# Attention scores over 128 rows: zero-padded queries in the memory of the residual

## The chip, the cores and the metric

The kernel runs on one core of a Trainium2 chip. The metric is the device time of one launch, in microseconds. Three runs of the kernel before took 1101.29, 1101.87 and 1102.76 us, a median of 1101.87.

## The reference

One decoder layer over 512 tokens of width 1024: a half-step feed-forward block with a layer norm, then two mixers side by side, then a projection with a second layer norm, then a second feed-forward block. What matters here is the attention mixer (4 heads; each has two maps with 64 query and key dimensions, and 128 value dimensions):

```python
def diff_attention_mixer(q, k, v, lq1, lk1, lq2, lk2, subln_w, lam_init, cos, sin):
    ...
    def block(args):
        qb, qp = args
        s = jnp.einsum("bqhmd,bkhmd->bhmqk", qb, k).astype(f32) * scale
        s = jnp.where(qp[:, None] >= pos[None, :], s, -jnp.inf)
        pr = jax.nn.softmax(s, axis=-1)
        attn = pr[:, :, 0] - lam * pr[:, :, 1]
        return jnp.einsum("bhqk,bkhd->bqhd", attn.astype(v.dtype), v)
...
        x = layer_norm(alpha * x + 0.5 * swiglu_ffn(x, ffn1_w13[i], ffn1_w2[i]), ln1_g[i], ln1_b[i])
        h = x @ w_in[i]
        ...
        x = layer_norm(alpha * x + mix @ w_out[i], ln2_g[i], ln2_b[i])
```

So `x` after the first layer norm is used twice: at once, by the projection into the mixers, and much later, as the residual of the second layer norm. In between nobody reads it in this layout.

## The kernel before

The 512 tokens are four tiles of 128 rows (`t` = 0 to 3). The residual lies in SBUF as four tiles `RES[t]` of 128 tokens x 1024 columns. Weight products are done in three passes over split operands (`mm3`, lines 291 to 293), from weights that SP loads into three buffers `raw` (L171), and that ACT and DVE split into a high and a low part (L159, L160); an output unit takes some 24 such passes. The small products of the mixers (scores, probabilities, delta rule) are plain f32 matmuls, each of which shows as two passes in the trace.

**First layer norm** (`norm_natural`, L296 to L328). At the end of the first block each tile gets its last sums (DVE, L471), statistics (DVE, L303 to L307), the power -1/2 on POOL (L308, L310), a scaling of the last 256 columns by ACT (L318) and two steps on those columns by POOL (L319, L320); DVE does the rest (L314, L323). PE transposes the tile (L335, `norm_turn`) after the last sums of the next one. After it `values_and_gates` projects the values; ACT copies them out of PSUM into `DV` (L896) and `AB` (L898).

**The mixers** (`mix_zone`) are written as lanes, generators that yield a modelled PE cost and a delay; `weave` takes them in the order of a modelled clock. The lanes are four of the delta rule (`gdn`), 16 of attention (4 tiles x 4 heads), the chain of states (`chain`), the output projections, and `fill`, which holds the long projections and is put between the others. What weave emits is then placed on the engines by a scheduler, which may move an instruction whose operands are ready far ahead of the place where it is written.

`fill` makes the keys and the queries: per tile a projection into PSUM, a copy by ACT (L983), the rotation on POOL (L876 to L880), four transposes on PE into PSUM (`turn4`, L841) and a copy by DVE into `DKT` or `DQT` (L973). Each holds 128 rows for a head: map 0 in rows 0 to 63, map 1 in rows 64 to 127.

`attention(t, h)` takes for each map the 64 rows of queries and keys as operands (L1129), adds the causal mask by a matmul over 128 rows (L1130), has DVE take the maximum (L1131), ACT the exponential (L1134), and DVE combine the maps (L1138). PE transposes the result (L1142), ACT copies it (L1144), PE multiplies it with the values (L1148), and the normalised result goes into `DQT`, over the queries that are used up (L1156).

`chain` has per chunk the products L1175 and L1183, L1190, a copy (L1192), L1200 and L1208, a norm, and the transposes of its result (L841 from `ta`). `out_attn` transposes the attention results and projects them, adding the residual (`RES`, L1245); `out_gdn` adds the other half and does the second layer norm.

Of the kernel before, what the change touches and what calls it, by code (L numbers as in the profile page):

```python
# [8 lines left out]
F32 = mybir.dt.float32  # L9
# [7 lines left out]
P = 128  # L17
D = 1024
S = 512
KT = D // P  # L20
NT = S // P
# [8 lines left out]
H = 4  # L30
# [5 lines left out]
DQK = 64  # L36
# [43 lines left out]
def bc(ap, axis, n):  # L80
    u = ap.unsqueeze(axis)
    shp = list(u.shape)
    shp[axis] = n
    return u.to_broadcast(shp)
# [29 lines left out]
class Layer:  # L114
# [39 lines left out]
    def ps(self, tag):  # L154
        return self.psp.tile([P, 512], F32, name=self.nm("p" + tag), tag=tag, bufs={"a": 3, "b": 2, "c": 3}[tag])
# [637 lines left out]
    def mix_zone(self, zone):  # L793
        tc, nc = self.tc, self.nc
        act, dve, pool, pe = nc.scalar, nc.vector, nc.gpsimd, nc.tensor
        XH, XL, RES, VEC, CONV = self.XH, self.XL, self.RES, self.VEC, self.CONV
        nm, cm, stat, ps, split, mm3 = self.nm, self.cm, self.stat, self.ps, self.split, self.mm3
        ident, idb, negb, mhalf, phalf = self.ident, self.idb, self.negb, self.mhalf, self.phalf
        mp = zone.enter_context(tc.tile_pool(name="mix", bufs=1))
# [6 lines left out]
        VV = mp.tile([P, NC, H, P], F32, name="VV")  # L806
        DV = mp.tile([P, NT, H, P], F32, name="DV")
        DKT = mp.tile([P, H, S], F32, name="DKT")
        DQT = mp.tile([P, H, S], F32, name="DQT")
        ST = [mp.tile([P, H, P], F32, name=f"ST{i}") for i in range(2)]  # L810
        ZG = MP[:, 0]
        g16 = [P, NC, H]
# [5 lines left out]
        LE4 = bc(cm(C_LE), 1, H)  # L818
        dp = zone.enter_context(tc.tile_pool(name="blocks", bufs=1, space=bass.MemoryType.DRAM))
        DM, DT, DU = (dp.tile([NC, H, 8, 16, 16], F32, name=f"blocks{i}") for i in range(3))  # L820
        pool.memset(TT, 0.0)
        said = set()

        def tmp(tag, bufs):
            return mp.tile([P, 512], F32, name=nm(tag), tag=tag, bufs=bufs)
# [4 lines left out]
        def tt():  # L830
            return tmp("tt", 3)

        def tb():
            return tmp("tb", 2)

        def v4(ap):
            return ap.rearrange("p (a b) -> p a b", b=P)

        def turn4(dst, src):
            for h in range(H):  # L840
                pe.transpose(dst[:, h * P:(h + 1) * P], src[:, h, :], ident)  # L841


        def block(t, w, pq, k0, k1):
            tk = slice(t * P, (t + 1) * P)
            for k in range(k0, k1):
                c = (k % 2) * 512
                mm3(pq, XH[:, k, tk], XL[:, k, tk], w[k // 2][0][:, c:c + 512], w[k // 2][1][:, c:c + 512],
                    k == 0, k == KT - 1)
                if t == NT - 1 and k % 2:  # L850
                    self.ahead()

        def columns(pq, w, k0, k1):
            wh, wl = w
            for k in range(k0, k1):
                mm3(pq, wh[:, k * P:(k + 1) * P], wl[:, k * P:(k + 1) * P], XH[:, k, :], XL[:, k, :],
                    k == 0, k == KT - 1)
            if k1 == KT:
                self.ahead()
# [103 lines left out]
                pool.tensor_tensor(NRM[:, c], q1[:, c], phalf[:, 0:H], ALU.pow)  # L963

        def fill():
            for dst, word in ((DKT, "k"), (DQT, "q")):
                w = [self.take() for _ in range(4)]
                held = None

                def turn(t, d):  # L970
                    pt = ps("b")
                    turn4(pt, v4(d))
                    dve.tensor_copy(dst[:, :, t * P:(t + 1) * P], v4(pt))  # L973
                    said.add((word, t))
                for t in range(NT):
                    pq = ps("b")
                    for i, (k0, k1) in enumerate(CUTS):
                        block(t, w, pq, k0, k1)
                        yield 0.65 * (k1 - k0), 0
                        if i == 1 and held:  # L980
                            turn(*held)
                    d = tb()
                    act.copy(d, pq)  # L983
                    rotary(d, t)
                    held = (t, d)
                yield 0, 0
                last = held
                if word == "k":
                    turn(*last)
                    yield 0.5, 0  # L990
            held = last
            for h in range(H):
                pq = ps("b")
                w = self.take()
                for i, (k0, k1) in enumerate(CUTS):
                    columns(pq, w, k0, k1)
                    yield 0.65 * (k1 - k0), 0
                    if i == 1 and h == 0:
                        turn(*held)
                    elif i == 1:  # L1000
                        self.v_turn(*held)
                vt = tb()
                conv(8 + h, pq, v4(vt))
                held = (h, vt)
            w = [self.take() for _ in range(4)]
            for t in range(NT):
                pq = ps("b")
                for i, (k0, k1) in enumerate(CUTS):
                    block(t, w, pq, k0, k1)
                    yield 0.65 * (k1 - k0), 0  # L1010
                    if t == 0 and i == 1:
                        self.v_turn(*held)
                        said.add("v")
                z = tb()
                act.activation(z, pq, AF.Silu)
                pool.tensor_tensor(ZG[:, t], v4(z), bc(VEC[:, V_NW:V_NW + P], 1, H), ALU.mult)
            said.add("z")
# [99 lines left out]
        def attention(t, h):  # L1117
            n = (t + 1) * P
            if t < 2:
                pc = ps("c")  # L1120
                sc = [pc[:, 0:n], pc[:, n:2 * n]]
            else:
                sc = [ps("c")[:, 0:n], ps("c")[:, 0:n]]
            mx = stat([P, 2], "amx")
            sm = stat([P, 2], "asm")
            pr = [tt()[:, 0:n], sc[1]]
            for m in range(2):
                r = slice(m * DQK, (m + 1) * DQK)
                pe.matmul(sc[m], DQT[r, h, t * P:(t + 1) * P], DKT[r, h, 0:n], start=True, stop=False)  # L1129
                pe.matmul(sc[m][:, n - P:n], idb, negb, start=False, stop=True)  # L1130
                dve.tensor_reduce(mx[:, m:m + 1], sc[m], AX.X, ALU.max)  # L1131
            dve.tensor_scalar(mx, mx, -SCALE, None, ALU.mult)
            for m in range(2):
                act.activation(pr[m], sc[m], AF.Exp, bias=mx[:, m:m + 1], scale=SCALE, accum_out=sm[:, m:m + 1])  # L1134
            rr = stat([P, 2], "arr")
            dve.reciprocal(rr[:, 0:1], sm[:, 1:2])
            dve.scalar_tensor_tensor(rr[:, 1:2], sm[:, 0:1], rr[:, 0:1], self.nlam, ALU.mult, ALU.mult)
            dve.scalar_tensor_tensor(pr[0], pr[1], rr[:, 1:2], pr[0], ALU.mult, ALU.add)  # L1138
            yield 0.2 + 0.43 * (t + 1), 4.5 + 0.8 * t
            pt = ps("c")  # L1140
            for c in range(t + 1):
                pe.transpose(pt[:, c * P:(c + 1) * P], pr[0][:, c * P:(c + 1) * P], ident)  # L1142
            at = tt()
            act.copy(at[:, 0:n], pt[:, 0:n])  # L1144
            yield 0.11 * (t + 1), 1.0 + 0.15 * t
            po = ps("c")
            for c in range(t + 1):
                pe.matmul(po[:, 0:P], at[:, c * P:(c + 1) * P], DV[:, c, h, :], start=c == 0, stop=c == t)  # L1148
            y = DQT[:, h, t * P:(t + 1) * P]
            so = stat([P, 4], "aso")  # L1150
            act.activation(y, po[:, 0:P], AF.Square, accum_out=so[:, 0:1])
            pool.tensor_tensor(so[:, 1:2], sm[:, 0:1], sm[:, 0:1], ALU.mult)
            dve.tensor_scalar(so[:, 2:3], so[:, 0:1], 1.0 / P, None, ALU.mult)
            dve.scalar_tensor_tensor(so[:, 2:3], so[:, 1:2], RMS_EPS, so[:, 2:3], ALU.mult, ALU.add)
            pool.tensor_tensor(so[:, 3:4], so[:, 2:3], mhalf[:, 0:1], ALU.pow)
            dve.scalar_tensor_tensor(y, po[:, 0:P], so[:, 3:4], VEC[:, V_SW:V_SW + P], ALU.mult, ALU.mult)  # L1156
            said.add(("attn", t, h))
            yield 0.22 * (t + 1), 0


        def to_mix(y, t, k0, tag):
            pt = ps(tag)
            turn4(pt, y)
            tk = slice(t * P, (t + 1) * P)
            split(XH[:, k0:k0 + 4, tk], XL[:, k0:k0 + 4, tk], v4(pt))
# [82 lines left out]

        def out_attn():
            for t in range(NT):  # L1250
                to_mix(DQT[:, :, t * P:(t + 1) * P], t, 4, "c")
                yield 0.5, 0
            w = [self.take() for _ in range(4)]
            for t in range(NT):
                yield from project_out(w, 0, t)
            said.add("out_attn")
# [15 lines left out]
        kq = keys_queries()  # L1272
# [123 lines left out]
```

## Time and profile before

| | |
|---|---|
| median of three runs | 1101.87 us (1101.29 to 1102.76) |
| the profiled execution, its own time | 1100.49 us |
| its span, first to last instruction | 1098.7 us |
| PE busy | 97% of the span |
| DVE, ACT, POOL busy | 76%, 44%, 10% |
| mean granted clock of PE | 0.997 of full speed |

The span is what the profiler saw between the first and the last instruction; the own time of that execution is 1.8 us more. Busy time of PE counts a matmul from its start to the modelled end of its pipeline, so neighbours overlap; the distance from one start to the next tells what a matmul takes. A line of the timeline that ends in x8 stands for eight equal instructions in a row, with the time from the first start to the last end. Brackets behind a line show how long the engine had been idle before, and what ended that. `64*128 64x512` reads: 64 rows by 128 columns of weights, 64 rows by 512 columns streamed.

### The profile page before, as it was taken

What the parts mean: (1) busy time and instruction counts of PE and PEld (TensorE: products, weight loads), DVE (VectorE), ACT (ScalarE), POOL (GpSimd) and SP (SyncE); (2) the same over time, 40 slices, a digit from 0 to 9 for tenths busy, and PEclk for the clock granted to TensorE, in tenths of its full rate; (3) what the DMA queues carried; (4) which work ended last, traced back from release to release, by engine and by line L of the source; (5) the groups of instructions that cost most, each with busy time, mean ns of one, the idle gap of its engine ahead of it and who ended that gap; (6) DMA issues with size and microseconds to landing.
All of it is one profiled execution on the core that took longest, in us unless ns stands there. A gap on an engine that the chain in (4) does not pass through costs nothing.

```text
span 1098.7 us, 17385 instructions
## 1 busy us (share of the span) xinstructions
PE 1070.0 (97%) x6627; PEld 942.1 (86%) x6627; DVE 829.8 (76%) x1446; ACT 488.7 (44%) x948; POOL 113.7 (10%) x175
## 2 busy tenths in 40 slices
PE   9899999999998999999999999999999999999997
PEld 7799898989897978777866787779999898999895
DVE  5988797879687465466765658899989695979577
ACT  5644353535352266324375632645545353535240
POOL 1100000000002302432111213100000000000003
PEclk9999999999999999999999999999999999999999
DMA  8623332333342042033210202434343332333212
GB/s 290 218 80 113 98 114 88 115 97 106 95 131 83 1 131 81 20 87 96 58 39 20 77 1 77 140 95 138 109 135 97 91 115 83 116 115 96 78 58 77
DMA packets 44275, 106.03 MB, mean 97 GB/s; under 512 B 10848, under 2 KB 12528, under 8 KB 44192
## 3 DMA queue, kind: packets, MB, share of 16 engines
q1 hardware_dynamic: 37968, 96.71, 28.9%
q0 software_dynamic: 1808, 6.04, 1.8%
q10 hardware_dynamic: 4416, 2.16, 0.7%
q8 instruction: 52, 0.85, 0.3%
q14 instruction: 31, 0.25, 0.1%
HBM read 102.41 MB, written 2.49 MB: 95 GB/s over the span
## 4 chain that ended last, share of the span: by engine, by line
PE 84%; DVE 7%; POOL 2%; DMA 2%; ACT 2%; issue 2%; DVEq 0%; ACTq 0%; POOLq 0%
PE pb L291 12%; PE pb L292 12%; PE pb L293 12%; PE pc L292 8%; PE pc L293 8%; PE pc L291 7%; PE pa L291 6%; PE pa L293 6%; PE pa L292 6%; PE pc L1129 2%; DVE wl L160 2%; DMA raw<-in_wa_dram 1%; ACT wh L159 1%; PE pa L1062 1%; DVE bnst L303 1%
## 5 line engine op out<-in xcount | busy, mean ns | idle before, releaser
L160 DVE TENSOR_TENSOR wl<-raw,wh 128x1024 fp32r<-128x1024 f32 (+3 forms) x137 | 144.0, 1057 | 37.5 <-ACT wh L159 36.5
L159 ACT CAST wh<-raw 128x1024 fp32r<-128x1024 f32 (+3 forms) x137 | 123.2, 904 | 95.3 <-PE pa L292 31.0
L291 PE MATMUL pb<-wh,hh 128*128 128x512 f32 (+1 forms) x356 | 138.6, 389 | 4.8 <-ACT hh L159 2.8
L292 PE MATMUL pb<-wl,hh 128*128 128x512 f32 (+1 forms) x356 | 137.8, 387 | 0.0
L293 PE MATMUL pb<-wh,hl 128*128 128x512 f32 (+1 forms) x356 | 137.8, 387 | 0.0
L223 ACT CAST th<-tr 128x512 fp32r<-128x512 f32 x160 | 98.4, 619 | 82.7 <-PE pc L292 48.4
L184 ACT CAST wh<-raw 128x512 fp32r<-128x512 f32 x88 | 54.7, 621 | 145.1 <-PE pb L293 93.6
L227 DVE TENSOR_TENSOR tl<-tr,th 128x512 fp32r<-128x512 f32 x160 | 109.3, 685 | 11.1 <-ACT th L223 10.3
L291 PE MATMUL pb<-wh,XH 128*128 128x512 f32 (+2 forms) x288 | 110.9, 385 | 2.3 <-ACT AB L898 0.6
L292 PE MATMUL pb<-wl,XH 128*128 128x512 f32 (+2 forms) x288 | 106.2, 369 | 1.0 <-DVE wl L160 0.9
L293 PE MATMUL pb<-wh,XL 128*128 128x512 f32 (+2 forms) x288 | 106.0, 368 | 0.0
L291 PE MATMUL pa<-XH,wh 128*128 128x256 f32 (+1 forms) x344 | 100.6, 292 | 3.8 <-ACT part L422 3.8
L292 PE MATMUL pa<-XL,wh 128*128 128x256 f32 (+1 forms) x344 | 100.3, 292 | 0.0
L293 PE MATMUL pa<-XH,wl 128*128 128x256 f32 (+1 forms) x344 | 100.3, 292 | 0.0
L185 DVE TENSOR_TENSOR wl<-raw,wh 128x512 fp32r<-128x512 f32 x88 | 60.5, 690 | 41.6 <-ACT wh L184 41.5
L291 PE MATMUL pc<-XH,th 128*128 128x256 f32 x320 | 90.6, 283 | 0.0
L292 PE MATMUL pc<-XL,th 128*128 128x256 f32 x320 | 90.6, 283 | 0.0
L293 PE MATMUL pc<-XH,tl 128*128 128x256 f32 x320 | 90.6, 283 | 0.0
L471 DVE TENSOR_TENSOR RES<-RES,pb 128x512 f32<-128x512 f32 (+1 forms) x81 | 54.9, 679 | 46.8 <-PE pb L293 45.9
L291 PEld LDWEIGHTS pb<-wh,hh 128*128 128x128 f32 x356 | 66.9, 188 | 19.7 <-ACT hh L159 3.2
L293 PEld LDWEIGHTS pb<-wh,hl 128*128 128x128 f32 x356 | 66.9, 188 | 14.0 <-DVE hl L160 0.4
L292 PEld LDWEIGHTS pb<-wl,hh 128*128 128x128 f32 x356 | 66.9, 188 | 13.1
(303 smaller groups left out, 2643.3 us busy)
## 6 DMA issues: line engine op xcount, KB each, us to landing
raw<-in_wa_dram SPq DMA_DIRECT2D x127, 512.0 KB, 3.7
raw<-in_wb_dram SPq DMA_DIRECT2D x88, 256.0 KB, 2.7
raw<-in_wd_dram SPq DMA_DIRECT2D x4, 520.0 KB, 3.7
RES<-in_xn_dram POOLq DMA_DIRECT2D x4, 512.0 KB, 6.9
gb<-in_gb_dram POOLq DMA_DIRECT2D x8, 256.0 KB, 5.1
xr<-in_xT_dram ACTq DMA_DIRECT2D x7, 256.0 KB, 4.6
out_dram<-RES SPq DMA_DIRECT2D x5, 256.0 KB, 2.1
TT<-in_gb_dram POOLq DMA_DIRECT2D x4, 256.0 KB, 3.6
```

Source lines behind the costliest of these rows:

```text
L159: self.nc.scalar.copy(hi, src)
L160: self.nc.vector.tensor_tensor(lo, src, hi.bitcast(F32), ALU.subtract)
L184: nc.scalar.copy(hi, r)
L185: nc.vector.tensor_tensor(lo, r, hi.bitcast(F32), ALU.subtract)
L223: act.copy(h, t)
L227: dve.tensor_tensor(hl[1], t, hl[0].bitcast(F32), ALU.subtract)
L291: pe.matmul(o, wh, xh, start=first, stop=False)
L292: pe.matmul(o, wh, xl, start=False, stop=False)
L293: pe.matmul(o, wl, xh, start=False, stop=last)
L303: dve.bn_stats(st[:, j, :], r[:, cuts[j]:cuts[j + 1]])
L471: dve.tensor_tensor(rj, rj, pd, ALU.add)
L1129: pe.matmul(sc[m], DQT[r, h, t * P:(t + 1) * P], DKT[r, h, 0:n], start=True, stop=False)
```

## The change

The queries get a place with 128 rows for each map, in which the other map's 64 rows are zero, so a score contracts over all 128 rows of `DKT`. That needs twice the space, 128 x 1024 for a tile, and the change takes `RES[t]` for it (`QZ[t]`, columns ordered by head, map and query). The residual is written to HBM (`XR`) at the start of the mixers and read back before the output projection, both by SP. Two copies on ACT place the two halves, instead of one copy by DVE; two memsets on POOL zero the rest. The results of the heads go into a tile of their own, `YB`, in place of `DQT`. The modelled PE cost of a head's scores goes from 0.43 to 0.22 us per key tile.

```diff
-        DQT = mp.tile([P, H, S], F32, name="DQT")
+        YB = mp.tile([P, H, S], F32, name="YB")
...
+        XR = dp.tile([NT, P, D], F32, name="XR")
+        for t in range(NT):
+            nc.sync.dma_start(XR[t], RES[t])
+        QZ = [RES[t].rearrange("p (h m b) -> p h m b", m=2, b=P) for t in range(NT)]
...
         def fill():
-            for dst, word in ((DKT, "k"), (DQT, "q")):
+            for word in "kq":
...
-                    dve.tensor_copy(dst[:, :, t * P:(t + 1) * P], v4(pt))
+                    if word == "k":
+                        dve.tensor_copy(DKT[:, :, t * P:(t + 1) * P], v4(pt))
+                    else:
+                        for m in range(2):
+                            r = slice(m * DQK, (m + 1) * DQK)
+                            act.copy(QZ[t][r, :, m, :], v4(pt)[r])
...
+                    if word == "q":
+                        pool.memset(QZ[t][DQK:, :, 0, :], 0.0)
+                        pool.memset(QZ[t][:DQK, :, 1, :], 0.0)
...
-                r = slice(m * DQK, (m + 1) * DQK)
-                pe.matmul(sc[m], DQT[r, h, t * P:(t + 1) * P], DKT[r, h, 0:n], start=True, stop=False)
+                pe.matmul(sc[m], QZ[t][:, h, m, :], DKT[:, h, 0:n], start=True, stop=False)
...
-            yield 0.2 + 0.43 * (t + 1), 4.5 + 0.8 * t
+            yield 0.2 + 0.22 * (t + 1), 4.5 + 0.8 * t
...
-            y = DQT[:, h, t * P:(t + 1) * P]
+            y = YB[:, h, t * P:(t + 1) * P]
...
         def out_attn():
             for t in range(NT):
-                to_mix(DQT[:, :, t * P:(t + 1) * P], t, 4, "c")
+                nc.sync.dma_start(RES[t], XR[t])
+            for t in range(NT):
+                to_mix(YB[:, :, t * P:(t + 1) * P], t, 4, "c")
```

Two places show how this moves instructions. The first is POOL in the first layer norm. `RES_69` to `RES_72` are the residual's four tiles, `bnrs` the statistics of a norm. Before:

```order
L319 TENSOR_TENSOR RES_69<-RES_69,gb_3790 128x256
L320 TENSOR_TENSOR RES_69<-RES_69,gb_3791 128x256
L308 TENSOR_TENSOR bnrs_3921<-bnrs_3921,mhalf 128x1
L310 TENSOR_SCALAR bnrs_3921<-bnmv_3919,bnrs_3921 128x1
L319 TENSOR_TENSOR RES_70<-RES_70,gb_3790 128x256
L320 TENSOR_TENSOR RES_70<-RES_70,gb_3791 128x256
L308 TENSOR_TENSOR bnrs_3979<-bnrs_3979,mhalf 128x1
```

With the change (L992 and L993 are the two memsets of a tile, in the new file's numbers):

```order
L319 TENSOR_TENSOR RES_69<-RES_69,gb_3790 128x256
L320 TENSOR_TENSOR RES_69<-RES_69,gb_3791 128x256
L992 MEMSET RES_69 64x4x128
L993 MEMSET RES_69 64x4x128
L308 TENSOR_TENSOR bnrs_3921<-bnrs_3921,mhalf 128x1
L310 TENSOR_SCALAR bnrs_3921<-bnmv_3919,bnrs_3921 128x1
L319 TENSOR_TENSOR RES_70<-RES_70,gb_3790 128x256
L320 TENSOR_TENSOR RES_70<-RES_70,gb_3791 128x256
L992 MEMSET RES_70 64x4x128
L993 MEMSET RES_70 64x4x128
L308 TENSOR_TENSOR bnrs_3979<-bnrs_3979,mhalf 128x1
```

The memsets of tiles 0, 1 and 2 stand between the norms of the tiles, and those of tile 3 behind the two memsets that follow the norm (of `TT` and `ta`). Each first memset waits for the tile's store to `XR` and for its transposes on PE.

The second place is PE behind the last score of the last head. Before, from that score's mask on:

```order
L1130 MATMUL pc_6149<-LVM,idb 128x128
L292 MATMUL pb_6175<-wl_5800,XH 128x512
...
L1148 MATMUL pc_6245<-DV,tt_6212 128x128 x4
...
L1190 MATMUL pa_6293<-VV,UU 128x128 x2
L841 MATMUL pc_6300<-CST,DQT 128x128 x4
L841 MATMUL pc_6307<-CST,DQT 128x128 x4
L841 MATMUL pc_6337<-CST,DQT 128x128 x4
L1200 MATMUL pa_6314<-ta_6298,KD 128x128 x4
L1208 MATMUL pa_6320<-ta_6298,MP 128x128 x4
```

With the change (L1153 is the old L1142, L1159 the old L1148, L1201 the old L1190, L1211 and L1219 the old L1200 and L1208, L845 the old L841):

```order
L1201 MATMUL pa_6291<-VV,UU 128x128
L1153 MATMUL pc_6236<-CST,tt_6151 128x128 x4
L1159 MATMUL pc_6264<-DV,tt_6241 128x128 x4
L1153 MATMUL pc_6321<-CST,tt_6222 128x128 x4
L1211 MATMUL pa_6298<-ta_6296,KD 128x128 x4
L1219 MATMUL pa_6304<-ta_6296,MP 128x128 x4
L1186 MATMUL pa_6328<-ST_4080,KQ 128x128 x4
L1194 MATMUL pa_6338<-ST_4080,KQ 128x128 x4
L1159 MATMUL pc_6347<-DV,tt_6326 128x128 x4
L845 MATMUL pc_6377<-CST,YB 128x128 x3
L1201 MATMUL pa_6359<-VV,UU 128x128 x4
L845 MATMUL pa_6366<-CST,ta_6316 128x128 x4
```

Before, 35 weight passes stood between the last score and the chain; now 15 do, the last two heads' products stand next to the chain's, and the first project passes come after its second chunk.

## Rows read from the trace of the kernel before

**Rows 1.** Page, part 1: engine, busy us, share of the span, instructions.

```profile
PE 1070.0 (97%) x6627; PEld 942.1 (86%) x6627; DVE 829.8 (76%) x1446; ACT 488.7 (44%) x948; POOL 113.7 (10%) x175
```

**Rows 2.** Windows: stretch, length, busy time of each engine, granted clock, DMA.

```profile
484.00:610.00 126.00, 123.81 (x684) 91.51 (x683) 81.44 (x217) 59.60 (x144) 22.66 (x50) 1.00 0.17 47
```

**Rows 3.** Timeline of PE at two 512-column scores: start, us, engine, line, tiles.

```profile
598.74 1.12 PE L1129 MATMUL pc<-DKT,DQT 64*128 64x512 f32 x2
...
600.15 0.40 PE L293 MATMUL pb<-wh,XL 128*128 128x512 f32 x1
600.47 1.12 PE L1129 MATMUL pc<-DKT,DQT 64*128 64x512 f32 x2
601.53 0.23 PE L1130 MATMUL pc<-LVM,idb 128*128 128x128 bf16 x1
```

**Rows 4.** Timeline of PE at a score of 128 columns.

```profile
499.59 0.48 PE L1129 MATMUL pc<-DKT,DQT 64*128 64x128 f32 x2
500.00 0.23 PE L1130 MATMUL pc<-LVM,idb 128*128 128x128 bf16 x1
```

**Rows 5.** Timeline of PE at the key products, f32 over 128 rows.

```profile
450.20 1.89 PE L1044 MATMUL pa<-KQ 128*128 128x256 f32 x8
451.92 0.27 PE L841 MATMUL pb<-CST,tb 128*128 128x128 f32 x1
```

**Rows 6.** Timeline of PE at two weight passes that follow each other.

```profile
490.46 0.39 PE L292 MATMUL pb<-wl,XH 128*128 128x512 f32 x1
490.69 0.40 PE L293 MATMUL pb<-wh,XL 128*128 128x512 f32 x1
```

**Rows 7.** Timeline of PE at f32 passes of 128 columns over 128 rows.

```profile
520.23 1.06 PE L1062 MATMUL pa<-TT,MP 128*128 128x128 f32 x8
521.12 0.60 PE L841 MATMUL pa<-CST,TT 128*128 128x128 f32 x4
```

**Rows 8.** Timeline of POOL in the first layer norm; idle time and its releaser in brackets.

```profile
352.18 0.99 POOL L308 TENSOR_TENSOR bnrs<-bnrs,mhalf 128x1 f32<-128x1 f32 x1 [2.07 <-DVE bnrs L307]
...
358.95 0.99 POOL L308 TENSOR_TENSOR bnrs<-bnrs,mhalf 128x1 f32<-128x1 f32 x1 [2.60 <-DVE bnrs L307]
...
365.29 0.99 POOL L308 TENSOR_TENSOR bnrs<-bnrs,mhalf 128x1 f32<-128x1 f32 x1 [2.17 <-DVE bnrs L307]
...
368.73 0.73 POOL L320 TENSOR_TENSOR RES<-RES,gb 128x256 f32<-128x256 f32 x1
```

**Rows 9.** Groups of POOL by shape: count, busy us, mean ns, idle before.

```profile
L615 POOL MEMSET zero<- 128x512 f32 x1 | 0.5, 524 | 0.3 <-POOLq L1385 0.3
```

**Rows 10.** DMA issues: tiles, queue, count, KB each, median us to landing.

```profile
raw<-in_wa_dram SPq DMA_DIRECT2D x127, 512.0 KB, 3.7
...
xr<-in_xT_dram ACTq DMA_DIRECT2D x7, 256.0 KB, 4.6
out_dram<-RES SPq DMA_DIRECT2D x5, 256.0 KB, 2.1
...
out_dram<-RES SPq DMA_DIRECT2D x6, 128.0 KB, 1.9
```

**Rows 11.** Timeline of ACT at the first copy of the value projection.

```profile
369.50 0.37 ACT L896 COPY DV<-pb 128x256 f32<-128x256 f32 x1 [1.67 <-POOL RES L320]
```

**Rows 12.** Timeline of PE at the value projection of the second tile.

```profile
369.99 0.39 PE L291 MATMUL pb<-wh,XH 128*128 128x264 f32 x1 [0.63 <-ACT AB L898]
```

**Rows 13.** Groups of ACT by shape, the copy of transposed probabilities.

```profile
L1144 ACT COPY tt<-pc 128x512 f32<-128x512 f32 x4 | 2.3, 585 | 0.0
```

**Rows 14.** Timeline of PE at the chain's first L1208.

```profile
621.56 1.06 PE L1208 MATMUL pa<-ta,MP 128*128 128x128 f32 x8
```

**Rows 15.** Timeline of DVE at the result of the chain's first chunk.

```profile
625.37 1.13 DVE L1222 SCALAR_TENSOR_TENSOR ta<-pa,gso,MP 128x128 f32<-128x128 f32 x4 [1.13 <-POOL gso L1219]
```

**Rows 16.** Timeline of SP around the first layer norm.

```profile
340.30 0.33 SPq L171 DMA_DIRECT2D raw<-in_wa_dram  x1
...
389.75 0.33 SPq L171 DMA_DIRECT2D raw<-in_wa_dram  x1
```

## The prediction

> **What bounds the kernel now.** I read the page's table of engines first: PE is busy for 97% of the span [rows 1], so I look for PE time, not for idle time elsewhere. The windows view then takes the stage in which the attention scores stand, 484 to 610 us: PE is busy for 123.8 of its 126 us there, at the full granted clock, while DVE, ACT and POOL all have room [rows 2]. A PE cost removed there should come off the end, unless a wait takes its place. The durations in the table of groups do not show what one matmul costs, because the matmuls overlap; the distances of starts in the timeline do, and I use those.
>
> Ordinary weight matmuls of 512 columns start 0.23 us apart [rows 6]. A score of 512 columns (two passes, one line of the timeline) goes like this [rows 3]: the weight matmul before it starts at 600.15 and would be through at 600.38; the score starts at 600.47, so 0.09 us are lost on the way in. From there to the mask matmul at 601.53 it takes 1.06 us.
>
> What should two passes take? The key products contract over 128 rows in the same precision: eight passes of 256 columns take 451.92 - 450.20 = 1.72 us, 0.215 us each [rows 5], so two passes of 512 columns take 0.86 us. The 64-row score is 0.20 us over that. A score of 128 columns takes 500.00 - 499.59 = 0.41 us [rows 4], against 0.22 us for two 128-row passes at (521.12 - 520.23) / 8 = 0.111 us [rows 7]: 0.19 us over. So the excess doesn't grow with the width: it is a price for entering and leaving, not for columns.
>
> **The change, part by part.** All sums are against the profiled execution, 1100.49 us, which is 1.38 us under the median of the three runs.
>
> *Scores over 128 rows.* There are 4 tiles x 4 heads x 2 maps = 32 score matmuls, and each loses 0.09 on the way in and 0.20 inside: 32 x 0.29 = **9.3 us** off PE. Lower end: only the part inside goes, 32 x 0.195 = 6.2; upper end 9.9, with the rounding of the rows. I take 9.3, since the 128-row f32 matmuls in the rows show neither loss. Zero rows add no columns, so the padding itself costs PE nothing.
> [...]
>
> *Zeroing the padding.* Eight memsets of 64 x 512 elements go to POOL, 0.52 us each by the row of the same length [rows 9], about 1.05 us a tile. The order puts those of tiles 0 to 2 not beside the queries but into the first layer norm, right behind L320 of their tile and ahead of L308 of the next tile. There they wait for the tile's store to HBM, because they overwrite what it reads, and the norm of the next tile stands behind them on POOL. This is the term that counts.
> POOL now idles 2.07, 2.60 and 2.17 us between L320 of one tile and L308 of the next, 6.84 in all [rows 8]. In its place comes: SP's wake-up (0.1), the store's landing, POOL's wake-up (0.1), the memsets (1.05). The store moves 512 KB from SBUF to HBM, which no row shows. Nearest are stores of 128 and 256 KB, 1.9 and 2.1 us, and loads of 512 KB, 3.7 us [rows 10]. The step from 128 to 256 KB is 0.2 for 128 KB more; with two to three such steps for the next 256 KB I take 2.7, nearer the stores, since it is one. That makes 3.95 us a tile: 3 x 3.95 - 6.84 = **5.0 us** later. With 2.1 it is 3.2, with 3.7 it is 8.0.
> Does PE feel it? Yes: the first copy of the value projection out of PSUM (L896) waits for the last L320, and PE waits for that copy, 0.63 us even now [rows 11, 12]; the copies begin at 369.50, right behind that L320, and PE goes on at 369.99. POOL also sets the pace: from one L308 to the end of L320 takes 4.17 us (365.29 to 368.73 + 0.73), with the new wait 8.1 us a tile, while DVE, which ends each gap today, comes round in at most 6.8 (352.18 to 358.95) [rows 8].
> [...]
>
> *Stores and reloads on SP.* The four stores stand between a weight load issued at 340.30 and one issued at 389.75 [rows 16]; SP has nothing else to do there, and they cost it nothing. Of the reloads, those of tiles 2 and 3 stand ahead of the fourth output-projection load and wait for the last scores. By the order some 45 rows of PE work, over 10 us, still lie between those scores and the matmul that needs the load, which lands in 3.7 [rows 10]: nothing while that cover stays, up to 3 us if the rows run together.
>
> *Queries turned by ACT.* Two copies replace one by DVE, 0.585 us each by a copy of that size [rows 13]. Six weight matmuls (1.4 us) stand between the transposes and the first score and cover the 1.2 us: nothing; without that cover at most 0.6 us for each of four tiles.
>
> *New order of the end.* The planner believes a head to cost PE 0.21 us per key tile less, so the heads move ahead and less projection work is left to put between the last heads and the delta-rule chain. In the new order L1148 (old numbers) of one head follows its L1142 with nothing between, so PE waits for the copy, 0.59 us [rows 13], and two hand-overs of about 0.1 each (L896 is over at 369.87, PE starts at 369.99 [rows 11, 12]): 0.8. And from the chain's first L1208 to the transposes of its result there are 35 passes at 0.111, 3.9 us of PE work, where the result now is ready at 625.37 + 1.13 = 626.50, 4.05 us after L1208's last pass (621.56 + 0.89) [rows 14, 15]: 0.2. Together **+1.0 us** (0, if other work slips between, to 3 with the two covers above gone).
>
> Sum: -9.3 + 5.0 + 1.0 = -3.3 on the profiled execution, and taken from the median 1101.87: **1098.6 us**. A measurement here tells 0.2%, 2.2 us, from no change.
>
> **The rivals.**
> 1. *The norm wait is small.* The store lands in 2.1 us and the end loses nothing: -9.3 + 3.2 = -6.1, 1095.8 us. For it: no other load runs beside these stores. Against: twice the bytes of the row.
> 2. *The heads can't use the freed PE.* Softmax on ACT and DVE becomes what the heads wait for, and half of the 9.3 returns: -4.6 + 5.0 + 1.0 = +1.4, 1103.3 us. For it: four more loads of ACT's function tables in the new order and PE waits at the scores already. Against: ACT and DVE are about half and two thirds busy [rows 2].
> 3. *Slower: the layer norm waits on the store.* If the store lands like the slow 256 KB load, 4.6 us [rows 10], a tile takes 5.85: 3 x 5.85 - 6.84 = 10.7, and -9.3 + 10.7 + 1.0 = +2.4, 1104.3 us. It decides from a landing of 3.8 us, where the gain is used up; 4.5 us makes it measurably slower. For it: a store of this size isn't in the trace. Against: all stores there land below loads of their size. [...]
> 4. *The change doesn't do what it says.* The loss comes from something else than the 64 rows and stays: 0 + 5.0 + 1.0 = +6.0, 1107.9 us. Against: 128-row f32 passes, in the same accumulation into PSUM, show none.
>
> **How the numbers follow.** The forecast has 0.50, rival 1 has 0.12, rival 2 has 0.20, rival 3 has 0.14, rival 4 has 0.04. The forecast sits only 1.1 us beyond the measurable limit, so I count 0.38 of its 0.50 as faster and 0.12 as the same. Faster: 0.38 + 0.12 = 0.50; same: 0.12 + 0.20 = 0.32; slower: 0.14 + 0.04 = 0.18. The range, 1095.0 to 1105.0 us, goes from just under rival 1 to just over rival 3; it leaves out rival 4 and the far ends of the unknown costs together (best -9.9 + 3.2, worst -6.2 + 8.0 + 3). The forecast's own range is 1096 to 1101.
>
> **What would show it.** Right: score rows of 128 x 128 with the mask 0.86 us behind a 512-column score, and no 0.09 in front; POOL's memsets in the layer norm with waits on the store before them and L320 of the last tile some 5 us later than 368.73; PE ahead by about 9 us between that point and the last score. Wrong: scores still 1.06 us long (rival 4); landings of XR well off 2.7 (rivals 1 and 3); PE idle at the scores or the transposes of the probabilities growing by microseconds (rival 2).

## The result, and the profile after

The changed kernel is slower: 1110.42 us, median of six runs (1104.82 to 1112.75), against 1102.35 (1101.29 to 1103.77) for the kernel before, a ratio of 1.007 (95% interval 1.005 to 1.0089). That is 8.1 us more where I forecast 3.3 less, and outside my range. The profiled execution is the fastest of the six, 1104.82 us (span 1103.0), so its trace explains only half of the loss: it is 4.3 us above the profiled execution of before. The six runs spread over 8 us, the six of before over 2.5.

PE is still what bounds it; ACT has more to do. The page, part 1 (as [rows 1]):

```profile
PE 1065.5 (97%) x6627; PEld 946.9 (86%) x6627; DVE 824.6 (75%) x1442; ACT 498.4 (45%) x960; POOL 116.2 (11%) x183
```

To find the place I cut the span where the same instruction stands in both kernels: POOL's setup for the first L308 (which itself runs some 16 us later), the last transposes of the first layer norm, the first score, and the first transposes of the second norm (columns as [rows 2]). The windows of the kernel before:

```profile
329.82:375.82 46.00, 42.24 (x257) 36.50 (x257) 30.28 (x58) 10.53 (x21) 15.06 (x18) 1.00 0.15 50
375.82:487.20 111.38, 107.93 (x540) 87.81 (x538) 56.11 (x99) 50.67 (x126) 28.29 (x41) 1.00 0.27 79
487.20:673.48 186.28, 182.22 (x1021) 140.93 (x1021) 119.41 (x290) 87.76 (x220) 36.51 (x64) 1.00 0.19 54
673.48:1098.70 425.22, 413.40 (x2709) 378.48 (x2707) 356.17 (x567) 182.56 (x308) 24.08 (x31) 1.00 0.33 100
```

The same four windows of the changed kernel:

```profile
328.88:381.27 52.39, 43.79 (x257) 37.78 (x257) 30.07 (x58) 10.64 (x21) 16.73 (x25) 0.97 0.23 84
381.27:492.57 111.30, 107.86 (x540) 88.02 (x539) 56.27 (x102) 51.83 (x128) 29.27 (x43) 1.00 0.26 79
492.57:678.76 186.19, 176.45 (x1021) 144.67 (x1020) 114.32 (x283) 96.17 (x230) 36.52 (x64) 0.99 0.22 66
678.76:1103.00 424.24, 413.44 (x2709) 378.41 (x2707) 355.95 (x567) 182.66 (x308) 23.89 (x31) 1.00 0.33 100
```

The stretch with the layer norm is 6.4 us longer. The stretch with the scores is as long as before, though PE is busy for 5.8 us less in it: what the scores gave was taken back by idle time (186.28 - 182.22 = 4.1 us before, 9.7 now) and by a clock below 1.00.

**The scores** did what the change says. PE's timeline at the two maps of a 512-column score, against [rows 3]:

```profile
603.74 1.02 PE L1140 MATMUL pc<-DKT,RES 128*128 128x512 f32 x2
604.60 0.22 PE L1141 MATMUL pc<-LVM,idb 128*128 128x128 bf16 x1
604.66 1.08 PE L1140 MATMUL pc<-DKT,RES 128*128 128x512 f32 x2
605.57 0.22 PE L1141 MATMUL pc<-LVM,idb 128*128 128x128 bf16 x1
```

From score to mask it is now 0.86 us, where it was 1.06. The second map, right behind the first one's mask, takes 0.91 (605.57 - 604.66).

**The layer norm.** POOL's timeline there, against [rows 8]:

```profile
344.49 1.00 POOL L308 TENSOR_TENSOR bnrs<-bnrs,mhalf 128x1 f32<-128x1 f32 x1 [15.60 <-DVE bnrs L307]
...
351.45 0.52 POOL L992 MEMSET RES<- 64x512 f32 x1 [2.77 <-DVE RES L314]
...
359.04 0.52 POOL L992 MEMSET RES<- 64x512 f32 x1 [2.81 <-DMA XR<-RES]
...
368.85 0.52 POOL L992 MEMSET RES<- 64x512 f32 x1 [5.04 <-DMA XR<-RES]
...
372.89 0.72 POOL L320 TENSOR_TENSOR RES<-RES,gb 128x256 f32<-128x256 f32 x1
```

The first two stores land as I took them, after 2.6 and 2.7 us. The third took 4.9 us. In the DMA view of the stretch from its issue to its landing (363.8 to 368.9 us; the queue lines give packets, MB and share) one thing stands beside it that the first store didn't have, a 16 KB packet of the queue that the view calls instruction:

```profile
q1 hardware_dynamic: 144, 0.52, 25.9%
q8 instruction: 1, 0.02, 2.1%
XR<-RES SPq DMA_DIRECT2D x1, 512.0 KB, 4.9
```

Packet by packet the trace shows the delay: the store has 128 packets of 4 KB and 16 of 4 bytes. Fifteen of the 4-byte packets are through by 366.1 us. The instruction packet lasts from 364.86 to 366.61; only from 366.59 on come the store's last eight 4 KB packets, one by one, and the last 4-byte packet at 368.24.

**PE's waits** (the view of waits for PE, 340 to 700 us: total, times, longest). The first is the layer norm's end, 0.6 us before [rows 12]; the next two are for ACT:

```profile
PE pb L291 <- ACT AB L902: 4.1, 1, 4.1
PE pa L1211 <- ACT ta L1203: 3.0, 1, 3.0
PE pb L845 <- ACT tb L873: 2.6, 1, 2.6
```

Before, the same view has no wait for the SiLU (L869 there, L873 now; the SiLU is an activation function that ACT computes), and 0.4 us at the chain's copy:

```profile
PE pa L1200 <- ACT ta L1192: 0.4, 1, 0.4
```

ACT's timeline ahead of the chain's copy L1203 shows what it was busy with. L1203 copies the chain's first product out of PSUM. The product (L1201) is through on PE at 616.2 us, and its copy starts 5.5 us later, behind two weight casts, a table load (1.28 us) and a SiLU:

```profile
617.64 2.00 ACT L159 CAST wh<-raw 128x1024 fp32r<-128x1024 f32 x2
...
619.92 1.28 ACT L1027 ACT_TABLE_LOAD   x1
621.21 0.60 ACT L1027 ACTIVATE tb<-pb 128x512 f32<-128x512 f32 x1
621.71 0.58 ACT L1203 COPY ta<-pa 128x512 f32<-128x512 f32 x1
```

Before, the copy (L1192) starts 1.1 us after the product (618.8 us), behind one SiLU without a table load and one cast:

```profile
618.49 0.60 ACT L1015 ACTIVATE tb<-pb 128x512 f32<-128x512 f32 x1 [0.39 <-PE pb L293]
618.99 1.04 ACT L159 CAST wh<-raw 128x1024 fp32r<-128x1024 f32 x1
619.92 0.59 ACT L1192 COPY ta<-pa 128x512 f32<-128x512 f32 x1
```

**The clock.** Windows of each of these three waits, in order of time, and of 3.4 us at the point where PE goes on, which is 374.14, 565.61 and 622.34 (the column behind POOL's is the granted clock):

```profile
370.00:373.50 3.50, 0.04 (x1) 0.00 (x0) 1.15 (x2) 0.60 (x1) 2.61 (x4) 1.00 0.00 0
373.60:377.00 3.40, 2.86 (x13) 2.86 (x14) 0.34 (x2) 0.72 (x3) 1.97 (x3) 0.50 0.39 157
562.98:565.61 2.63, 0.00 (x1) 0.00 (x0) 1.86 (x3) 2.60 (x4) 0.00 (x0) 1.00 0.01 3
565.70:569.10 3.40, 3.40 (x19) 2.50 (x20) 2.66 (x7) 1.08 (x4) 0.55 (x1) 1.00 0.44 154
619.40:622.30 2.90, 0.00 (x0) 0.00 (x0) 2.20 (x5) 2.87 (x7) 0.89 (x2) 1.00 0.47 107
622.80:626.20 3.40, 3.40 (x19) 3.40 (x18) 0.00 (x0) 1.00 (x4) 1.44 (x2) 0.50 0.43 166
```

Behind the first and the last wait PE runs at a granted clock of 0.50: the matmuls of 264 columns behind the first wait start 0.22 us apart until 376.95 us, and 0.12 apart from 377.11 on, where the clock is 1.00. The last such stretch loses 1.7 us, the first 1.4, since PE goes on only 0.5 us into it. Behind the middle wait it didn't happen in this execution. The mean granted clocks of the six runs, in the order of their times, are 0.994, 0.989, 0.992, 0.988, 0.991 and 0.988.

So the theories. **N**: the wait in the layer norm carries the loss. **O**: the order that follows from the cost 0.22 does. **C**: the clock behind the waits is a cost of its own.

### The profile page after: what moved, and what is told of

It reads as the page before. It is cut to its first block, busy times and chain, and to the rows that moved or that the text cites. A ratio compares the mean times of both kernels' runs of the same rounds, so it can differ in the third digit from the quotient of the medians.

```text
span 1103.0 us, 17414 instructions
## 1 busy us (share of the span) xinstructions
PE 1065.5 (97%) x6627; PEld 946.9 (86%) x6627; DVE 824.6 (75%) x1442; ACT 498.4 (45%) x960; POOL 116.2 (11%) x183
## 4 chain that ended last, share of the span: by engine, by line
PE 77%; DVE 8%; DMA 5%; ACT 3%; POOL 3%; issue 2%; SPq 0%; DVEq 0%; POOLq 0%; ACTq 0%
PE pb L291 12%; PE pb L292 11%; PE pb L293 11%; PE pc L293 7%; PE pc L291 7%; PE pc L292 7%; PE pa L291 5%; PE pa L292 5%; PE pa L293 5%; DMA raw<-in_wa_dram 3%; DVE wl L160 2%; ACT wh L159 2%; PE pc L1140 1%; PE pa L845 1%; PE pa L1074 1%
## 5 line engine op out<-in xcount | busy, mean ns | idle before, releaser
L159 ACT CAST wh<-raw 128x1024 fp32r<-128x1024 f32 (+3 forms) x137 | 123.1, 905 | 100.5 <-PE pa L292 30.8
```

The lines of the kernel that those rows point to most:

```text
L159: self.nc.scalar.copy(hi, src)
```

## The experiments

Each was timed beside runs of the kernel before on the same chip; "against before" is the difference of the two medians in us.

| run | median us | against before | ratio (95%) |
|---|---|---|---|
| the change | 1110.42 | +8.1 | 1.007 (1.005 to 1.0089) |
| scaled_copies | 1103.55 | +1.7 | 1.0009 (0.9998 to 1.002) |
| old_cost | 1102.80 | +1.0 | 1.0009 (0.9999 to 1.0019) |
| scaled_copies_old_cost | 1099.29 | -2.5 | 0.998 (0.9968 to 0.9993) |
| before_new_cost | 1111.07 | +9.3 | 1.0078 (1.006 to 1.0097) |
| no_store | 1102.43 | +1.3 | 1.0016 (1.0004 to 1.0028) |
| filled_gap | 1108.12 | +7.0 | 1.0057 (1.0041 to 1.0074) |
| scaled_cost_033 | 1101.49 | +0.4 | 1.0005 (0.9996 to 1.0013) |
| scaled_cost_052 | 1098.97 | -2.1 | 0.9978 (0.9966 to 0.9989) |
| scaled_cost_062 | 1098.41 | -2.2 | 0.9979 (0.997 to 0.9989) |
| late_turn_043 | 1097.15 | -3.5 | 0.9971 (0.9959 to 0.9983) |
| late_turn_052 | 1098.01 | -2.6 | 0.9978 (0.9969 to 0.9986) |
| before_late_turn | 1104.00 | +3.4 | 1.0025 (1.0008 to 1.0043) |
| filled_all | 1105.19 | +4.3 | 1.0036 (1.0022 to 1.005) |
| filled_before_new_cost | 1103.98 | +3.1 | 1.0023 (1.0012 to 1.0034) |
| filled_052 | 1097.38 | -3.6 | 0.9966 (0.9954 to 0.9977) |

### The layer norm and the order, apart and together

**scaled_copies**: the padding comes out of the copies on ACT, with no memsets. `C_LE` and `C_GT` are constants whose column 63 is 1 in rows 0 to 63, or in rows 64 to 127.

```diff
-                        for m in range(2):
-                            r = slice(m * DQK, (m + 1) * DQK)
-                            act.copy(QZ[t][r, :, m, :], v4(pt)[r])
+                        for m, o in enumerate((C_LE, C_GT)):
+                            act.activation(QZ[t][:, :, m, :], v4(pt), AF.Copy, scale=cm(o + DQK - 1, 1))
...
-                        pool.memset(QZ[t][DQK:, :, 0, :], 0.0)
-                        pool.memset(QZ[t][:DQK, :, 1, :], 0.0)
```

> The padding is made by the two ACT copies themselves, scaled per row by 1 or 0 over all 128 rows; the eight POOL memsets are gone, so nothing in the first layer norm waits for the stores. Theory N (the wait in the layer norm carries the loss): about 6.9 us of it lay in the norm and the rest of the change brings its 8.3, so about 1102.4 - 8.3 = 1094 us. Theory O (the order that follows from the cost 0.22 eats the gain, the norm adds its 6.9 on top): 1110.4 - 6.9 = 1103.5 us, with the two PE waits of 2.6 and 3.0 us on ACT still there.

**old_cost**: `0.2 + 0.43 * (t + 1)` again in place of `0.2 + 0.22 * (t + 1)`.

> The changed kernel with the planner's cost back at 0.43; the memsets stay. Theory N: the order was worth 1 us, about 1109 us. Theory O: the 9.3 us of the scores come through and only the norm is lost, 1102.4 - 9.3 + 6.9 = 1100 us, and the two waits of 2.6 and 3.0 us are gone.

**scaled_copies_old_cost**: both edits.

> Scaled copies in place of the memsets, and the cost back at 0.43. Both theories: nothing is left but the gain of the scores, 1102.4 - 9.3 = 1093 us. If it stays above 1098, a third cost is at work (the stores and reloads, or the copies on ACT).

**before_new_cost**: the kernel before with the one number changed.

```diff
-            yield 0.2 + 0.43 * (t + 1), 4.5 + 0.8 * t
+            yield 0.2 + 0.22 * (t + 1), 4.5 + 0.8 * t
```

> The kernel before with 0.22 in place of 0.43 and nothing else, so only the order changes. Theory N: within 1 or 2 us of 1102.4. Theory O: slower by 4 us or more, 1106 to 1110 us, with new PE waits on ACT behind weight casts and table loads.

Theory O holds in kind, N alone falls. O's sizes were off: old_cost is 2.8 us above its sum, before_new_cost 1 us above its range. One number, with no other edit, costs the kernel before 9.3 us, and its two long waits in the mixers are those of the changed kernel to the tenth:

```profile
PE pa L1200 <- ACT ta L1192: 3.0, 1, 3.0
PE pb L841 <- ACT tb L869: 2.6, 1, 2.6
```

Windows of the two waits and of what follows each, same kernel:

```profile
564.10:566.70 2.60, 0.01 (x1) 0.01 (x1) 1.81 (x2) 2.57 (x4) 0.00 (x0) 1.00 0.02 6
568.30:575.10 6.80, 6.80 (x18) 4.23 (x17) 3.96 (x12) 3.16 (x7) 0.74 (x2) 0.50 0.09 37
626.40:629.40 3.00, 0.05 (x2) 0.00 (x1) 2.30 (x5) 2.97 (x7) 0.93 (x2) 1.00 0.45 117
629.70:633.10 3.40, 3.40 (x18) 3.40 (x17) 0.00 (x0) 0.86 (x3) 1.59 (x2) 0.50 0.50 177
```

Here the clock fell behind both, 10.2 us at half clock. In the changed kernel the order is worth 7.1 us (+8.1 against +1.0), the memsets 6.4 (+8.1 against +1.7); without the memsets the order is worth only 4.2 (+1.7 against -2.5). So the costs don't simply add.

One part of such totals has nothing to do with the change. Every kernel has a PE wait for ACT (`hh`, L159) of 2.2 to 4.2 us near 340 us, ahead of the layer norm. In 13 of the 17 profiles PE ran at half clock for 3.4 or 6.8 us behind it, in before_new_cost for 6.8; in the profiles of the kernel before and of the change it didn't. That is why I compare profiles stretch by stretch.

Both edits together gave -2.5, not the -9.3 expected: a third cost. In the profile of scaled_copies_old_cost, from the first score to the second norm, PE is busy for 6.7 us less than before and idle for 3.8 us more, and the clock is at half for 3.4 us of it:

```profile
490.49:673.88 183.39, 175.50 (x1022) 143.78 (x1021) 114.83 (x283) 91.35 (x227) 35.73 (x64) 0.99 0.23 67
```

One wait makes most of that, at the transposes that wait for the SiLU:

```profile
PE pb L845 <- ACT tb L873: 3.8, 1, 3.8
```

old_cost, with the same number but with the memsets, has no such wait, and its clock stays up there. The same stretch is 5.05 us shorter than in the kernel before:

```profile
494.44:675.67 181.23, 174.82 (x1021) 142.90 (x1020) 114.77 (x283) 90.98 (x226) 37.08 (x64) 1.00 0.23 68
```

So the wait comes with the order that the scaled copies bring at this number; which of its moves makes it wasn't tried.

### Is it the stores or the memsets

**no_store**: the changed kernel without the lines of `XR` (four stores, four reloads).

> The changed kernel without the stores to XR and the reloads; the memsets stay where they are. It leaves out the residual of the second layer norm. Theory S (the wait in the first layer norm is for the stores' landing): the memsets now run as soon as the tile's transposes are through, the next tile's norm waits for DVE as before, PE goes on behind the value projection's first tile with less than 1.2 us of idle time, and the time is that of the scaled copies at the same cost, 1103.5 us. Theory M (the memsets themselves, POOL time in a chain that POOL paces): 3 x 1.05 us stay, about 1107 us.

It goes to the level of the scaled copies, 1102.4 us, as theory S says, and PE's wait behind the first tile is 0.9 us. POOL's timeline at the memsets of the first tile shows why the memsets cost next to nothing by themselves: they are through before DVE has the next tile's statistics. It is the same at the two other tiles.

```profile
352.61 0.52 POOL L990 MEMSET RES<- 64x512 f32 x1 [1.04 <-PE pa L335]
353.19 0.52 POOL L991 MEMSET RES<- 64x512 f32 x1
354.71 0.93 POOL L308 TENSOR_TENSOR bnrs<-bnrs,mhalf 128x1 f32<-128x1 f32 x1 [1.00 <-DVE bnrs L307]
```

The late store came again. Twelve of the profiled kernels have the stores. In ten of them a 16 KB instruction packet falls into the flight of one of the first three stores, and that one lands after 4.3 to 5.1 us. In the two others (scaled_copies, filled_052) the packet falls between stores, and none of the three is late. Of the first three stores, all without such a packet land after 2.6 or 2.7 us. I didn't try to move the instruction packets.

### Other costs, and the SiLU

**scaled_cost_033**, **scaled_cost_052**, **scaled_cost_062**: scaled copies with that number in place of 0.22.

> Scaled copies with a planner's cost of 0.33. Theory T (the cost spaces the heads, and with heads closer together ACT's queue makes PE wait): between the 1099.3 of 0.43 and the 1103.5 of 0.22, about 1101.5 us. Theory L (each value gives another order, and the waits fall as they fall): anywhere from 1094 to 1106 us, with the long waits at other places.

> Scaled copies with a planner's cost of 0.52. Theory T: heads further apart, shorter waits, 1094 to 1098 us. Theory L: anywhere from 1094 to 1106 us.

> Scaled copies at the cost 0.62. Theory T (heads further apart, shorter waits): 1097 to 1099 us, no better than 0.52 if the wait for the SiLU stays. Theory L: anywhere from 1094 to 1106 us.

At 0.33 PE has the same two waits of 3.0 and 2.6 us as at 0.22; at 0.52 and 0.62 the one of 3.8 us as at 0.43. So the number doesn't space the heads evenly: five values gave two patterns of long waits. Theory T got the times nearly right (0.52 and 0.62 no better than 0.43 within the intervals, 0.33 between) for a reason that the waits don't bear out.

**late_turn_043**, **late_turn_052**, **before_late_turn**: the transposes behind the SiLU are written later, in scaled copies at either cost, and in the kernel before.

```diff
-                    elif i == 1:
+                    elif i == 2 and h > 0:
                         self.v_turn(*held)
...
-                    if t == 0 and i == 1:
+                    if t == 0 and i == 2:
```

> Scaled copies at the cost 0.43, and the transposes of the value convolution's result are written after the third part of the next projection, not after the second, two weight blocks (six passes) later. Theory W (what is left of the loss is one PE wait of 3.8 us for the SiLU, which stands behind other heads' exponentials and a table load on ACT, and 1.7 us at half clock behind it): the wait falls under 2.4 us or goes, the clock stays, 1099.3 - 1.4 - 1.7 = about 1096 us, 1094 if the wait goes altogether. Rival R (the PSUM buffer that the transposes need later takes the place of the wait): 1099 us or more.

> The same move at the cost 0.52. Theory W: 1099.0 - 3.1 = about 1096 us, 1093.5 if the wait goes altogether. Rival R: 1099 us or more.

> The same move alone in the kernel before, whose PE does not wait for that SiLU. Theory W: nothing to gain, 1101 to 1103 us. If it is faster by more than 2 us, the move helps for a reason that has nothing to do with the scores.

The wait for the SiLU is gone in both runs with scaled copies; in its place PE waits 1.9 us for the PSUM buffer that the transposes now hold longer (late_turn_043):

```profile
PE pb L291 <- DVE VV L1030: 2.4, 2, 1.9
```

The clock stays at 1.00 there. The move gained 1.0 us at 0.43 and 0.5 at 0.52, between W and R; the intervals overlap, so neither gain is shown. In the kernel before the same move costs 3.4 us, where W expected no change. Its profile has the same wait for that buffer, 1.8 us long, and PE at half clock from 0.3 us behind it:

```profile
557.40:567.60 10.20, 10.20 (x23) 6.02 (x22) 4.80 (x13) 5.08 (x11) 0.65 (x3) 0.50 0.15 50
```

From the first score to the second norm it takes 189.8 us, 3.5 more than the kernel before.

### Filling the waits

**filled_gap**: 18 matmuls that nobody reads, in the layer norm's wait; they write to a PSUM buffer that is free there.

```diff
+                if t == 1:
+                    pf = ps("c")
+                    for _ in range(18):
+                        pe.matmul(pf[:, 0:384], w[3][0][:, 0:P], XH[:, 0, 0:384], start=True, stop=True)
```

> The changed kernel with 18 matmuls of 384 columns, whose result nobody reads, put on PE between the value projections of the first and the second tile, where PE stood idle for 4.09 us; they take about 18 x 0.17 = 3.1 us. Theory C (idle PE lowers the granted clock and that costs on top of the wait): the wait stays as long, but the matmuls behind it start 0.11 us apart at once, granted clock 1.00; 1.7 us less, 1108.7 us. Rival (the slow matmuls behind the gap have another cause, or the filler delays the work by its own length): 1110.4 us or more.

**filled_all**: these, and the two waits for ACT filled as well (`self.turned` is the last transpose of the last head). **filled_before_new_cost** has the two in the kernel before at cost 0.22; **filled_052** has the first of them, with 14 matmuls, in scaled copies at 0.52.

```diff
             pt = ps("b")
+            if h == 1:
+                for _ in range(9):
+                    pe.matmul(pt, XH[:, 0, 0:P], XH[:, 0, :], start=True, stop=True)
...
                     pk = ps("a")
+                    if c == 0:
+                        with tc.issue_after(self.turned.ins):
+                            for _ in range(11):
+                                pe.matmul(pk, XH[:, 0, 0:P], XH[:, 0, :], start=True, stop=True)
```

> The changed kernel with matmuls that nobody reads in its three long PE waits: 18 of 384 columns between the value projections (idle 4.09 us), 9 of 512 ahead of the transposes that wait for the SiLU (2.63 us), 11 of 512 behind the last transposes of probabilities, ahead of the chain's wait for its copy (2.95 us). Theory C (the granted clock falls behind idle stretches): the waits last as long as before, no half-clock stretch follows them, the clocks of the runs rise from 0.988 to 0.994 to 0.995 or more, and the median falls by 5 us or more, to 1102 to 1105 us, with a smaller spread. Rival (the excess over the waits has another cause, such as the late stores): 1108 us or more, and the spread stays.

> The kernel before with the cost 0.22, and the two fillings of the mixers (9 and 11 matmuls). In its profile 10.2 us behind the two waits ran at half clock, 5.1 us lost. Theory C: 1111.1 - 5.1 = 1106 us. Rival: 1110 us or more.

> Scaled copies at the cost 0.52 with 14 matmuls of 512 columns ahead of the transposes that wait for the SiLU (3.76 us idle). Theory C: 1.7 us less in the runs that had a half-clock stretch there, so 1097.3 to 1098 us where it was 1099.0. Rival: 1099 us or more.

Work that nobody reads makes the kernel faster. In the kernel before at 0.22 it takes 6.2 us off (+9.3 to +3.1). The mean granted clock of its runs rises from 0.990 to 0.996, the kernel before's own level (0.995 in both sessions): by these clocks, times the runs' lengths, some 6.4 us less were lost to half clock, about the whole gain. In the changed kernel the fillings take 3.8 us off (+8.1 to +4.3), and the mean granted clock goes from 0.990 to 0.996. Its six runs spread over 1.6 us, where those of the change spread over 8; that is a weak sign, since the kernel before spreads over 4.6 to 6.3 in 22 to 30 runs. Of the two waits for ACT 0.6 and 1.4 us are left, and the clock behind both is whole (windows of filled_all: filling and what follows, for either wait):

```profile
564.50:567.50 3.00, 2.45 (x12) 1.88 (x10) 2.15 (x4) 2.97 (x5) 0.00 (x0) 1.00 0.01 3
567.50:571.00 3.50, 3.48 (x19) 2.58 (x20) 2.64 (x7) 1.19 (x4) 0.55 (x1) 1.00 0.52 154
618.70:624.20 5.50, 4.18 (x26) 3.41 (x24) 3.98 (x8) 5.38 (x11) 0.84 (x2) 1.00 0.55 181
624.20:627.60 3.40, 3.33 (x29) 3.33 (x30) 0.39 (x3) 2.24 (x11) 1.99 (x2) 1.00 0.59 223
```

Theory C holds for the waits in the mixers. For the layer norm's wait alone (filled_gap, 1.1 us less) the intervals overlap, and its profile and that of filled_all don't show the case that the filling was made for. In both, the second store was the late one. PE then waited earlier, at the transposes, and ran at half clock for 3.4 us behind that; it reached the filling only when ACT could already copy (filled_all, PE and then ACT; L904 and L906 are the old L896 and L898):

```profile
366.60 0.44 PE L335 MATMUL pa<-CST,RES 128*128 128x128 f32 x2 [1.48 <-POOL RES L320]
374.13 3.29 PE L894 MATMUL pc<-XH,wh 128*128 128x384 f32 x18
374.14 0.38 ACT L904 COPY DV<-pb 128x256 f32<-128x256 f32 x1 [1.67 <-POOL RES L320]
```

The last copy that PE needs (L906) is through at 374.6, and PE goes on at 377.3, so there the filling delayed the work by some 2.6 us. Whether it helps when the third store is the late one stays open.

filled_052 gains 1.5 us on its unfilled twin, as expected, though the intervals overlap; it and late_turn_043 are the fastest of all, 3.5 us below the kernel before.

## Why the prediction was wrong

- **Scores, -9.3**: right in kind, sized a little high. Without the idle time and without the 1.7 us lost to half clock, PE's work between the first score and the second norm fell from 182.2 to 176.45 - 1.7 = 174.7 us: 7.5. In old_cost, which has no half clock there, it fell to 174.8: 7.4. Where the maps' scores stand back to back, the second is 0.05 us longer.
- **Zeroing the padding, +5.0**: the mechanism was right, and the price by some luck. From the first L308 to the end of the last L320 it now takes 372.89 + 0.72 - 344.49 = 29.1 us, where it took 368.73 + 0.73 - 345.92 = 23.5: 5.6 more. The first two stores landed in the 2.7 us I took. Two things weren't in my sum and work against each other: the third one's extra 2.2 us, and 0.45 us that POOL's own steps are shorter in each of three tiles (L308 takes 0.55 us behind the memsets, 0.99 before). Rival 3's point, 3.8 us, was passed by one store of three. Of that store's 4-byte packets fifteen were through by 366.1 us, and the sixteenth came at 368.24, behind the eight 4 KB packets that followed the 16 KB packet; that this packet held them up is how I read the times, and no run moved it. No row shows the two wake-ups of 0.1 us a tile in my sum: in the changed kernel SP's issue starts 0.03 us behind L320, and the memset 0.14 us behind the landing.
- **New order of the end, +1.0, at most 3**: the step that failed. I looked at PE's rows and the covers between them, and found two small ones. I didn't look at ACT's order, where weight casts, a table load and a SiLU slid ahead of the copy that the chain waits for, and a head's exponentials and a cast ahead of another SiLU that PE waits for. PE's idle time in the stretch grew by 5.7 us (4.1 to 9.7), where I had 1.0, and the number alone cost the kernel before 9.3 us, clock included. The 0.8 us of my sum, PE waiting for the copy of a head's probabilities, came as 0.7. I had written that moved heads leave less work for the end; what they did was to bunch ACT's work.
- **What was in no term**: the clock. My sum took a wait at its length. In the profiled run the half clock behind two waits cost another 3.1 us. In the runs it cost more, by an estimate from the clocks: the mean of the six granted clocks is 0.990, that of the profiled one 0.994; 0.4% of 1103 us is 4.4 us of the 5.6 by which the median lies above the profiled run. Nor does the same wait always bring it: the change and filled_gap have the same mixers and the same wait of 2.63 us, followed by full clock in the profile of the one and by 3.4 us at half clock in that of the other.
- **Stores and reloads on SP, 0; queries turned by ACT, 0**: nothing in the waits speaks against either. scaled_copies keeps the stores and reloads and no_store leaves them out, at +1.7 and +1.3, which don't differ clearly; the copies on ACT weren't tried alone.
- **Rival 2** (the heads can't use the freed PE) named ACT, but the wrong place: PE waits at the chain's copy and at a SiLU, not for the heads' softmax. It said half the gain returns; with what the clock added, all of it did. Even in the best version 3.5 of 7.5 us are left.

By the profiled run: -7.5 (scores) + 5.7 (waits) + 1.7 (clock) in the mixers, + 6.4 (1.4 of it clock) in the layer norm, -0.1 between the two, and -1.0 in the second block, 5.2 us in all, as the two tables of windows give (774.1 - 768.9). The stretch ahead of them, which the change doesn't touch, was 0.9 us shorter, which leaves the 4.3 us between the profiled executions.

## What to carry to other kernels

A planner's number that is brought closer to the truth for one engine can still make the order worse, because the order also sets what queues up on the others: time the number alone, and read the new order of the engine that PE waits for, not only PE's. An idle stretch on PE cost its length here and, in some profiles, a stretch at half clock behind it, from 3.4 us (the change, behind waits of 4.1 and 3.0 us) to 10.2 us (before_late_turn, behind 1.8 us); a mean granted clock below that of the kernel before was the sign (0.990 for the change; 0.995 to 0.996 for the kernel before, over 22 to 30 runs). Padding that can come out of an existing copy, by a scale of 0 or 1 per row, needs no memset that waits for a store.

## What I had not expected of the hardware

- 20 matmuls that nobody reads, put into two waits of 2.6 and 3.0 us, took 6.2 us off the time.
- A 512 KB store to HBM landed in 2.6 to 2.7 us, and in 4.3 to 5.1 in the ten profiles' one store that had a 16 KB instruction packet beside it.
- The same wait of 2.63 us stands in six profiles: full clock followed in three (the change, scaled_copies, scaled_cost_033), half clock for 3.4 or 6.8 us in three (filled_gap, no_store, before_new_cost).
- A wait of 1.8 us was followed by 10.2 us at half clock in the kernel before with late transposes; one of 1.9 at the same place, in the two other kernels with that move, by none.
